# A two-layer encoder trunk: gate evacuation on ScalarE with the bias added on GpSimd, and an earlier hook for the next norm's transposes

## The chip, the cores and the metric

The kernel runs on one core of one Trainium2 chip. The metric is the device time of one execution in microseconds (us), the median of several runs. The engines are named as in the profile: PE (TensorE, with PEld for its weight loads), DVE (VectorE), ACT (ScalarE), POOL (GpSimd) and SP (SyncE, which issues DMAs here).

## The reference

Two layers, each a half-step feed-forward block, a mixer of three gated branches, and a second half-step feed-forward block, with a final norm at the end. All data is float32; the sequence has 256 tokens of 1024 channels. Cut to what matters here:

```python
for i in range(DEPTH):                      # DEPTH = 2
    h = rms_norm(x, ffn1_norm[i])
    x = x + 0.5 * swiglu_ffn(h, ffn1_w_gate[i], ffn1_w_up[i], ffn1_w_down[i])

    h = rms_norm(x, mix_norm[i])
    # one projection of h feeds three branches: S5, GLA, attention
    gates = jax.nn.sigmoid(h @ w_merge_gate[i] + b_merge_gate[i])     # 1024 x 3072
    gates = gates.reshape(bsz, seq_len, N_BRANCHES, D_MODEL)
    merged = (gates[:, :, 0] * (y_s5 @ w_branch_s5[i])
              + gates[:, :, 1] * (y_gla @ w_branch_gla[i])
              + gates[:, :, 2] * (y_attn @ w_branch_attn[i]))
    x = x + merged @ w_out[i]

    h = rms_norm(x, ffn2_norm[i])
    x = x + 0.5 * swiglu_ffn(h, ffn2_w_gate[i], ffn2_w_up[i], ffn2_w_down[i])
return rms_norm(x, final_norm)
```

## The kernel before

The 256 tokens are two tiles `t` of 128 partitions. Each large product is made of three matmuls (`mm3`, lines 219 to 221): activations and weights are each split into a rounded part and a remainder, and high times high, high times low and low times high are summed in PSUM. Weights are streamed: `load` fetches pieces of two times 128 rows by 512 columns into `raw`, ACT casts them to `hi` (L209), DVE subtracts to get `lo` (L210), and PE uses both. `raw`, `hi` and `lo` have five buffers each.

`stream` walks over weight blocks of 512 columns and over chunks of the contraction; when a block's last chunk is done, it calls the block's `evac` for both token tiles. `hooks` are calls put in after a chunk.

The norms are folded: `Norm.half` transposes x on PE (`pt`, L1127) and splits it into `hTh` and `hTl` without the root; each evacuation multiplies by the root `rstd`, one value for each token, that is for each partition.

In the mixer the main sequence (`MAIN`) runs input projection, the three gate streams g0, g1, g2, then the branch projections and the output projection `merge`. `weave` puts steps of the three branches between its chunks: these are the many small DVE, ACT and PE instructions around the gate streams (scans L790, L791, L908 and L909, products with tables L300, exponentials L920 and L921, transposes such as `goT`, L969, of the first GLA outputs). A gate block is evacuated by `ev` in `gate_stream`: DVE computes `ps * rstd + bm` (L714; `bm` is the bias, sent to all partitions by a DMA), ACT applies tanh in place (L715). A gate tile is 128 by 512; there are 12 in each mixer, 24 in the program.

The order on each engine is not that of the code. A scheduler places the instructions by a model of their times, and each engine then works through its own queue in that fixed order. An instruction that waits holds back all behind it on its engine.

## Time and profile before

| | |
|---|---|
| median of 3 runs | 1339.02 us (1336.95 to 1339.86) |
| profiled execution, its own time | 1340.2 us |
| its span, first to last instruction | 1338.4 us |
| granted TensorE clock, mean over the span | 0.996 |
| busy: PE, DVE, ACT, POOL | 1301.7, 1001.8, 700.9, 80.3 us |
| the two mixers' gate streams | about 320 to 397 us and 978 to 1055 us |

The busy sums are over the whole span. What matters for the change is the stretch of the gate streams, where the balance of the engines is another one than in the feed-forward blocks.

### The profile page before, as it was taken

How to read it: one execution, taken by the hardware profiler on the slowest of the kernel's cores; microseconds unless marked ns; L12 is line 12 of the kernel's file. 1: busy time of each engine (PE TensorE's matmuls, PEld its weight loads, DVE VectorE, ACT ScalarE, POOL GpSimd, SP SyncE). 2: the span in 40 equal slices, each digit the busy share in tenths (PEclk: the TensorE clock that was granted, in tenths of full speed). 3: DMA queues.
4: the chain of work that ended last, by engine and by line, in shares of the span. 5: the costliest groups of instructions: out<-in, count | busy, mean ns of one | idle time of the engine just before them, and what ended most of it. 6: DMA issues, size and time to landing. Idle time of an engine off the chain costs nothing.

```text
span 1338.4 us, 19258 instructions
## 1 busy us (share of the span) xinstructions
PE 1301.7 (97%) x6792; PEld 1050.6 (78%) x6792; DVE 1001.8 (75%) x1794; ACT 700.9 (52%) x1130; POOL 80.3 (6%) x108
## 2 busy tenths in 40 slices
PE   7999999999999999999999999999999999999997
PEld 5888778877787678888887888887787867788886
DVE  5899995779997769999556775557899966655553
ACT  5455444547675455544444454463485853645542
POOL 1010221000100000101000100000001000000000
PEclk9999999999999999999999999999999999999999
DMA  7766676676463367676656655576555525555561
GB/s 233 199 207 214 241 245 179 198 232 206 145 201 114 114 163 197 194 254 216 199 170 213 201 184 198 175 205 199 192 194 189 169 69 170 171 181 186 195 197 59
DMA packets 201200, 249.87 MB, mean 187 GB/s; under 512 B 40856, under 2 KB 134600, under 8 KB 201104
## 3 DMA queue, kind: packets, MB, share of 16 engines
q1 hardware_dynamic: 200496, 247.59, 59.1%
q8 instruction: 53, 0.87, 0.3%
q10 hardware_dynamic: 608, 1.06, 0.2%
q14 instruction: 43, 0.35, 0.1%
HBM read 234.44 MB, written 13.11 MB: 185 GB/s over the span
## 4 chain that ended last, share of the span: by engine, by line
PE 67%; issue 17%; DVE 11%; DMA 3%; POOL 1%; ACT 1%; SPq 0%; POOLq 0%; ACTq 0%; DVEq 0%
PE mm L219 19%; PE mm L221 19%; PE mm L220 19%; DVE lo L210 3%; DVE t L300 1%; DMA raw<-in_ffn_w_up 1%; PE S L773 1%; DMA e<-scr 1%; PE st L274 1%; PE as L1025 1%; PE ao L1047 1%; DVE run L791 1%; PE yp L811 1%; PE pt L1127 1%; PE apt L1040 1%
## 5 line engine op out<-in xcount | busy, mean ns | idle before, releaser
L210 DVE TENSOR_TENSOR lo<-raw,hi 128x1024 fp32r<-128x1024 f32 x412 | 499.4, 1218 | 203.6 <-ACT hi L209 193.6
L209 ACT CAST hi<-raw 128x1024 fp32r<-128x1024 f32 x412 | 427.8, 1043 | 330.2 <-PE mm L221 261.2
L219 PE MATMUL mm<-hi,hTh 128*128 128x512 f32 (+1 forms) x1120 | 441.8, 397 | 5.2 <-ACT hTh L1131 3.6
L220 PE MATMUL mm<-lo,hTh 128*128 128x512 f32 (+1 forms) x1120 | 441.1, 395 | 3.3 <-DVE lo L210 3.0
L221 PE MATMUL mm<-hi,hTl 128*128 128x512 f32 (+1 forms) x1120 | 429.7, 392 | 0.5 <-DVE hTl L1132 0.5
L219 PEld LDWEIGHTS mm<-hi,hTh 128*128 128x128 f32 x1120 | 211.1, 189 | 49.3 <-ACT hTh L1131 5.2
L220 PEld LDWEIGHTS mm<-lo,hTh 128*128 128x128 f32 x1120 | 211.5, 189 | 45.7 <-DVE lo L210 4.9
L221 PEld LDWEIGHTS mm<-hi,hTl 128*128 128x128 f32 x1120 | 210.9, 189 | 42.0 <-DVE hTl L1132 0.9
L220 PE MATMUL mm<-lo,sThffn 128*128 128x512 f32 x352 | 138.5, 394 | 2.2 <-DVE lo L210 2.2
L221 PE MATMUL mm<-hi,sTlffn 128*128 128x512 f32 x352 | 138.0, 393 | 0.0
L219 PE MATMUL mm<-hi,sThffn 128*128 128x512 f32 x352 | 137.1, 395 | 0.0
L220 PEld LDWEIGHTS mm<-lo,sThffn 128*128 128x128 f32 x352 | 66.5, 189 | 17.5 <-DVE lo L210 3.5
L219 PEld LDWEIGHTS mm<-hi,sThffn 128*128 128x128 f32 x352 | 66.6, 189 | 13.7
L221 PEld LDWEIGHTS mm<-hi,sTlffn 128*128 128x128 f32 x352 | 66.4, 189 | 14.0
L276 ACT CAST sThffn<-st 128x256 fp32r<-128x256 f32 x88 | 31.4, 373 | 73.0 <-PE st L274 72.6
L270 ACT ACTIVATE t<-mm,rstd 128x256 f32<-128x256 f32 x88 | 41.2, 473 | 49.0 <-PE mm L221 46.9
L277 DVE TENSOR_TENSOR sTlffn<-st,sThffn 128x256 fp32r<-128x256 f32 x88 | 35.8, 418 | 33.0 <-ACT sThffn L276 33.0
L271 DVE SCALAR_TENSOR_TENSOR t<-mm,rstd,t 128x256 f32<-128x256 f32 x88 | 41.0, 478 | 12.1 <-ACT t L270 11.8
L578 POOL COPY kx<-ks 128x128 f32<-128x128 f32 x32 | 24.0, 791 | 218.5 <-DVE ks L561 172.8
L300 DVE TENSOR_TENSOR t<-e,S 128x512 f32<-128x512 f32 x32 | 20.3, 682 | 15.0 <-DMA e<-scr 12.2
L274 PE MATMUL st<-ident,t 128*128 128x128 f32 x176 | 31.5, 273 | 0.0
L274 PEld LDWEIGHTS st<-ident,t 128*128 128x128 f32 x176 | 23.3, 140 | 9.1
(354 smaller groups left out, 1417.6 us busy)
## 6 DMA issues: line engine op xcount, KB each, us to landing
raw<-in_ffn_w_gate SPq DMA_DIRECT2D x176, 256.0 KB, 3.6
raw<-in_ffn_w_up SPq DMA_DIRECT2D x176, 256.0 KB, 3.8
raw<-in_ffn_w_down SPq DMA_DIRECT2D x88, 512.0 KB, 4.7
raw<-in_w_in SPq DMA_DIRECT2D x48, 512.0 KB, 3.8
raw<-in_w_merge_gate SPq DMA_DIRECT2D x48, 512.0 KB, 4.8
raw<-in_w_out SPq DMA_DIRECT2D x16, 512.0 KB, 3.8
scr<-e SPq DMA_DIRECT2D x6, 768.0 KB
e<-scr SPq DMA_DIRECT2D x6, 768.0 KB, 5.4
```

What stands on the lines that cost most here:

```text
L209: nc.scalar.copy(hi[:, :e - s, :width], raw[:, :e - s, :width])
L210: nc.vector.tensor_tensor(lo[:, :e - s, :width], raw[:, :e - s, :width], hi[:, :e - s, :width].bitcast(F32), op=ALU.subtract)
L219: nc.tensor.matmul(ps, act[0], w[0], start=first, stop=False)
L220: nc.tensor.matmul(ps, act[0], w[1], start=False, stop=False)
L221: nc.tensor.matmul(ps, act[1], w[0], start=False, stop=last)
L270: nc.scalar.activation(sg, ps[:, :256], AF.Silu, scale=rstd[:, t:t + 1])
L271: nc.vector.scalar_tensor_tensor(s, ps[:, 256:], rstd[:, t:t + 1], sg, op0=ALU.mult, op1=ALU.mult)
L274: nc.tensor.transpose(pt[:, j], s[:, j * P:(j + 1) * P], self.ident)
L276: nc.scalar.copy(h, pt)
L277: nc.vector.tensor_tensor(sl[:, 2 * b:2 * b + 2, t * P:(t + 1) * P], pt, h.bitcast(F32), op=ALU.subtract)
L300: self.nc.vector.tensor_tensor(out, a, b, op=ALU.mult)
L578: nc.gpsimd.tensor_copy(kx[:, :, s], ks.rearrange("p g j f -> p g (j f)")[:, :, (3 - s) * 16:(3 - s) * 16 + 64])
```

## The change

Three edits.

1. The gate's `scalar_tensor_tensor` on DVE is replaced by two instructions: ACT copies the PSUM tile with `rstd` as its scale, and POOL adds the bias in place. The tanh on ACT stays, and now waits for POOL.
2. The bias tile `bm` gets two buffers, where it had one.
3. `stream` also calls hooks with a key (chunk, sub-chunk), and the output projection's last hook, the first half of the next norm (`nm.half(0)`), is called after the first half of the last chunk's matmuls and no longer after all of them.

```diff
@@ stream
                 for t in range(NT):
                     for k in range(k0 + s, min(k1, k0 + s + SUB)):
                         self.mm3(ps[b, t][:, :width], act(k, t), w[k - k0], k == 0, k == nk - 1)
+                if (i, s) in hooks:
+                    hooks[i, s]()
             if i in hooks:
                 hooks[i]()
@@ gate_stream
-            bm = self.mp.tile([P, 512], F32, name=self.nm("bm"), tag="bm")
+            bm = self.mp.tile([P, 512], F32, name=self.nm("bm"), tag="bm", bufs=2)
...
                 g = gates[i][:, t, cs]
-                nc.vector.scalar_tensor_tensor(g, ps, rstd[:, t:t + 1], bm, op0=ALU.mult, op1=ALU.add)
+                nc.scalar.activation(g, ps, AF.Copy, scale=rstd[:, t:t + 1])
+                nc.gpsimd.tensor_tensor(g, g, bm, op=ALU.add)
                 nc.scalar.activation(g, g, AF.Tanh, scale=0.5)
@@ merge
-                               lead=2, hooks={0: lambda: mg.half(1), 3: lambda: nm.half(0)})
+                               lead=2, hooks={0: lambda: mg.half(1), (3, 0): lambda: nm.half(0)})
```

The scheduler sees the edits and places anew. Outside the mixers nothing moves. The lines of the changed kernel are two or three higher than before (L718 is the tanh there).

The first gate, on ACT, in the first mixer; `mm_3356` and `mm_3357` are the two token tiles of the first gate block, `gate_0` the gate. Before:

```order
L915 ACTIVATE mid_3160<-t_3157 128x1 x2
L814 COPY yg_2613<-yp_3215 128x2x4x16
L814 COPY yg_2613<-yp_3216 128x2x4x16
L918 ACTIVATE end_3161<-la_3077 128x1
L209 CAST hi_3721<-raw_3719 128x1024
L715 ACTIVATE gate_0_3339<-gate_0_3339 128x512
```

Now:

```order
L918 ACTIVATE mid_3160<-t_3157 128x1
L716 ACTIVATE gate_0_3339<-mm_3356,rstd_1795 128x512
L918 ACTIVATE mid_3160<-t_3157 128x1
L817 COPY yg_2613<-yp_3215 128x2x4x16
L817 COPY yg_2613<-yp_3216 128x2x4x16
L718 ACTIVATE gate_0_3339<-gate_0_3339 128x512
L921 ACTIVATE end_3161<-la_3077 128x1
L716 ACTIVATE gate_0_3339<-mm_3357,rstd_1795 128x512
L209 CAST hi_3725<-raw_3723 128x1024
```

The first tanh now stands ahead of the cast of the next weight piece (`hi_3721` before, `hi_3725` now), with only two short copies and one tiny activation between it and its evacuation; the second evacuation stands behind it.

DVE, some 25 us later in the same mixer, where the weight pieces of the second gate are made beside the S5 scans (L790 and L791 before, L793 and L794 now). Before:

```order
L714 SCALAR_TENSOR_TENSOR gate_0_3339<-mm_3525,rstd_1795,bm_3342 128x512
L210 TENSOR_TENSOR lo_3805<-raw_3802,hi_3804 128x1024
L210 TENSOR_TENSOR lo_3873<-raw_3870,hi_3872 128x1024
L303 TENSOR_TENSOR t_3322<-t_3322,t_3323 128x512
L306 TENSOR_TENSOR t_3324<-t_3324,t_3325 128x512
L210 TENSOR_TENSOR lo_3879<-raw_3876,hi_3878 128x1024
L985 TENSOR_REDUCE ass_3419<-t_3424 128x2
L790 SCALAR_TENSOR_TENSOR run_2590<-e_3305,t_3322 64x511
L791 SCALAR_TENSOR_TENSOR run_2590<-e_3305,t_3322 64x511
L300 TENSOR_TENSOR t_3416<-sp_3489,cst 128x256
L790 SCALAR_TENSOR_TENSOR run_2590<-e_3305,t_3324 64x511
L791 SCALAR_TENSOR_TENSOR run_2590<-e_3305,t_3324 64x511
```

Now:

```order
L793 SCALAR_TENSOR_TENSOR run_2590<-e_3305,t_3322 64x511
L794 SCALAR_TENSOR_TENSOR run_2590<-e_3305,t_3322 64x511
L793 SCALAR_TENSOR_TENSOR run_2590<-e_3305,t_3324 64x511
L794 SCALAR_TENSOR_TENSOR run_2590<-e_3305,t_3324 64x511
L210 TENSOR_TENSOR lo_3885<-raw_3882,hi_3884 128x1024
L988 TENSOR_REDUCE ass_3419<-t_3427 128x8
L302 TENSOR_TENSOR t_3416<-sp_3491,cst 128x256
L796 MEMSET run_2590 64x16
L797 MEMSET run_2590 64x16
L210 TENSOR_TENSOR lo_3982<-raw_3979,hi_3981 128x1024
```

The piece that was `lo_3879`, ahead of the scans, is now `lo_3885`, behind them; the piece after it (`lo_3976` before, `lo_3982` now) follows with a reduction and a small product between. The four gate instructions that stood ahead of the scans on DVE are gone.

PE, where the first GLA outputs are transposed (`goT_3400`). Before:

```order
L221 MATMUL mm_3883<-hi_3981,hTl_1798 128x512
L219 MATMUL mm_4074<-hi_4064,hTh_1797 128x512
L220 MATMUL mm_4074<-lo_4065,hTh_1797 128x512
L221 MATMUL mm_4074<-hi_4064,hTl_1798 128x512
L219 MATMUL mm_4074<-hi_4064,hTh_1797 128x512
L969 MATMUL goT_3400<-ident,t_3168 128x128 x2
```

Now:

```order
L220 MATMUL mm_3889<-lo_3885,hTh_1797 128x512
L221 MATMUL mm_3889<-hi_3884,hTl_1798 128x512
L221 MATMUL mm_3888<-hi_3981,hTl_1798 128x512
L972 MATMUL goT_3400<-ident,t_3168 128x128
L936 MATMUL keT_3487<-ident,la_3077 128x128
L972 MATMUL goT_3400<-ident,t_3168 128x128
```

The transposes stood at row 1525 of PE's queue and now stand at row 1503: 22 matmuls earlier, in the middle of the second gate's last chunk and no longer in the third gate's first.

The third edit moves nothing. Built with it and without it (the other two edits alike), the queues of all five engines have the same instructions at the same places; only the numbers in the names of the transposes' buffers differ (`pt_4812` with it, `pt_4824` without it). The eight transposes of x stand behind the last matmul of the output projection either way.

## Rows read from the trace of the kernel before

**Rows 1.** Page, busy us (share of the span) and instructions of each engine

```profile
PE 1301.7 (97%) x6792; PEld 1050.6 (78%) x6792; DVE 1001.8 (75%) x1794; ACT 700.9 (52%) x1130; POOL 80.3 (6%) x108
```

**Rows 2.** Windows: length, busy us of PE, PEld, DVE, ACT, POOL, clock

```profile
320.00:350.00 30.00, 30.00 (x184) 24.89 (x183) 29.66 (x44) 21.92 (x43) 0.54 (x1) 1.00 0.58 194
350.00:380.00 30.00, 27.61 (x161) 21.73 (x160) 29.76 (x49) 16.86 (x37) 4.26 (x2) 1.00 0.56 177
...
1007.00:1037.00 30.00, 27.58 (x161) 21.64 (x160) 29.79 (x48) 16.79 (x36) 4.24 (x2) 1.00 0.55 180
```

**Rows 3.** PE's waits, 320 to 370 us: total us, times, longest

```profile
PE mm L220 <- DVE lo L210: 1.5, 1, 1.5
PE mm L219 <- DVE gate L714: 0.8, 1, 0.8
```

**Rows 4.** Timeline of PE: start us, duration us, instruction, idle before

```profile
353.62 0.39 PE L221 MATMUL mm<-hi,hTl 128*128 128x512 f32 x1
353.85 0.39 PE L219 MATMUL mm<-hi,hTh 128*128 128x512 f32 x1
355.72 0.50 PE L220 MATMUL mm<-lo,hTh 128*128 128x512 f32 x1 [1.49 <-DVE lo L210]
...
366.46 0.38 PE L969 MATMUL goT<-ident,t 128*128 128x128 f32 x2
```

**Rows 5.** Timeline of DVE at the first gate

```profile
325.08 1.20 DVE L210 TENSOR_TENSOR lo<-raw,hi 128x1024 fp32r<-128x1024 f32 x1
...
326.53 1.22 DVE L210 TENSOR_TENSOR lo<-raw,hi 128x1024 fp32r<-128x1024 f32 x1
327.67 0.74 DVE L714 SCALAR_TENSOR_TENSOR gate<-mm,rstd,bm 128x512 f32<-128x512 f32 x1
328.33 0.42 DVE L306 TENSOR_TENSOR la<-t 128x256 f32<-128x256 f32 x1
...
329.32 1.21 DVE L210 TENSOR_TENSOR lo<-raw,hi 128x1024 fp32r<-128x1024 f32 x1
```

**Rows 6.** Timeline of DVE from the scans to the first GLA output

```profile
349.15 1.20 DVE L790 TENSOR_TENSOR_SCAN run<-e,t 64x511 f32<-64x511 f32 x1
...
355.58 0.68 DVE L985 TENSOR_REDUCE ass<-t 128x8 f32<-128x512 f32 x1
...
356.51 1.22 DVE L210 TENSOR_TENSOR lo<-raw,hi 128x1024 fp32r<-128x1024 f32 x1
...
363.69 0.61 DVE L966 SCALAR_TENSOR_TENSOR t<-go,grs,gs 128x128 f32<-128x128 f32 x2
```

**Rows 7.** Timeline of ACT at the first gate

```profile
324.45 0.20 ACT L915 ACTIVATE mid<-t 128x1 f32<-128x1 f32 x1
...
326.81 1.03 ACT L209 CAST hi<-raw 128x1024 fp32r<-128x1024 f32 x1
328.44 0.63 ACT L715 ACTIVATE gate<-gate 128x512 f32<-128x512 f32 x1 [0.60 <-DVE gate L714]
```

**Rows 8.** Groups by line: busy us, mean ns, idle before

```profile
L714 DVE SCALAR_TENSOR_TENSOR gate<-mm,rstd,bm 128x512 f32<-128x512 f32 x24 | 17.7, 745 | 0.0
...
L671 ACT ACTIVATE gs<-mm,rstd 128x512 f32<-128x512 f32 x2 | 1.4, 686 | 0.0
...
L568 POOL TENSOR_TENSOR e<-r,tcst 128x512 f32<-128x512 f32 x8 | 17.6, 2202 | 178.1 <-DVE r L300 105.1 <-DMA scr<-e 54.2 <-DVE T L316 11.1
```

**Rows 9.** Timeline of POOL and DVE, two executions of POOL's L568

```profile
157.70 2.65 POOL L568 TENSOR_TENSOR e<-r,tcst 128x512 f32<-128x512 f32 x1 [11.07 <-DVE T L316]
...
159.37 0.41 DVE L277 TENSOR_TENSOR sTlffn<-st,sThffn 128x256 fp32r<-128x256 f32 x1
159.71 1.73 DVE L210 TENSOR_TENSOR lo<-raw,hi 128x1024 fp32r<-128x1024 f32 x1
...
537.65 1.06 POOL L568 TENSOR_TENSOR e<-r,tcst 128x512 f32<-128x512 f32 x1 [48.00 <-DVE r L300]
...
537.70 1.07 DVE L319 TENSOR_TENSOR pt<-pw 128x32 f32<-128x32 f32 x1
```

## The prediction

> **What bounds the kernel now.** I began with the page: PE is busy 1301.7 of 1338.4 us [rows 1], so a change on DVE, ACT or POOL can shorten the time only by what PE waits, and lengthen it by any wait that it adds. Then I cut the gate streams into windows [rows 2]. From 320 to 380 us DVE is busy 29.66 and 29.76 of 30 us, ACT only 21.92 and 16.86, POOL 0.54 and 4.26; the second mixer reads the same (29.79 from 1007 to 1037 us). DVE is full there, and the edit takes work from it. But PE's waits in that stretch are small: 1.5 us for a `lo` and 0.8 us for a PSUM tile that a gate still holds [rows 3], 2.3 us in a mixer and 4.6 us in both. That is all that this stretch can give back. The wait for `lo` stands at 355.72 us, where PE had been ready since about 354.1 [rows 4].
>
> **What the change removes.** 24 gate instructions of 745 ns leave DVE [rows 8]. In DVE's full queue each is worth the step to the next start, 327.67 to 328.33 = 0.66 us [rows 5]; 12 in a mixer make 7.9 us. Four of them stand ahead of the late `lo`. DVE had no idle time before any gate [rows 8]: the tiles lie complete while DVE is behind, so ACT can take them at once, and PE's 0.8 us wait should go.
>
> **What it adds on ACT.** 24 copies from PSUM with a per-partition scale. The same form with the same shape is L671, 686 ns [rows 8]: 8.2 us in a mixer, and ACT has 8.1 and 13.1 us free in the two windows [rows 2]. As mere work this is hidden. It is the order that is not: ACT's first tanh stands between the first evacuation and the next cast, so while it waits for POOL, the second evacuation, the GLA steps and the cast of the next weight piece wait too, and behind that cast DVE's whole queue, whose next instruction is that piece's `lo`.
>
> **What it adds on POOL.** 24 adds of 128x512 with both inputs in SBUF. The nearest row is L568, a POOL TENSOR_TENSOR of that shape: 2202 ns on average over eight [rows 8], but 1.06 us where it was quick [rows 9]. The two executions shown tell why. At 157.70 POOL was ready, DVE was in a chain of products with two SBUF inputs, and POOL finished at 160.35: the work of 1.06 us can only have begun at about 159.3, when DVE came to L277 (159.37), whose one input is in PSUM. The DVE instruction after it, L210 with two SBUF inputs, then took 1.73 us, where it takes 1.20 to 1.22 elsewhere [rows 5, 9]; at 537.70 a small DVE product beside POOL took 1.07 us. I read from this that a POOL add waits while DVE runs two-input SBUF work without a gap, and that a DVE instruction of that kind waits while POOL adds. Bounds for the add's latency: 1.06 us, and several times that; for what it costs DVE: nothing (when DVE waits anyway or has a PSUM input) to about 0.9 us (537.70). I take 0.65 us where DVE is working, between 1.73 - 1.21 = 0.5 and 0.9. That is what the gate cost it before: **DVE's relief is paid back**.
>
> The Trainium skill's page "SBUF — State Buffer", section "Who interferes with whom", says that a DVE instruction with two SBUF inputs contends with a GpSimd instruction that reads SBUF, and that whoever issues first holds the shared ports for its whole instruction. The mutual hold agrees with rows 9; a wait of one instruction at most, as first come first served would have it, does not, since POOL stood behind more than one there. By the page's rule the first add would go in when the running `lo` ends at 326.3, DVE's next piece would start at 329.75, each later add would hold DVE for about 0.9, and the sum below would read 329.75 + 17.4 + 2.7 = 349.85 for the scans, 358.1 for `lo_3982` and 365.5 for L966: 4.1 us late in a mixer, +8 us in place of +5.7.
>
> **The sum, in the first mixer, on the clock of the rows.** ACT's first `mid` ends at 324.65 [rows 7], the evacuation at about 325.3. DVE then runs L909, `lo` (325.08), `la`, `lo` (326.53), `la`, all with two SBUF inputs, until about 328.0, when it needs the piece whose cast stands behind the tanh. Only now POOL gets in: add to 329.1, tanh to 329.75, `end` 0.1, second evacuation 0.6, cast 1.03 [rows 7]: DVE's next `lo` starts at 331.5. Before it started at 329.32 [rows 5]. From there to the scans DVE took 349.15 - 329.32 = 19.8 us [rows 5, 6]; take off two gates (1.3) and the `lo` that now follows the scans (1.14, the step 326.53 to 327.67): 17.4. Of adds 2 to 4, the second falls mostly into DVE's wait for the cast (0.2), the third holds a product for 0.65, and the fourth lies beside the products with S, which is in PSUM (0): 0.85. The scans begin at 331.5 + 17.4 + 0.85 = 349.75. Four scans of 1.21 [rows 6], the `lo` 1.15, the reduction and the small products 1.05, the next `lo` 1.15 bring `lo_3982` to 358.0. From that `lo`'s end (357.73) to the end of L966, the input of `goT`, DVE took 6.6 us before [rows 6]; without the two gates between and with one small copy moved in (0.3) it is 5.6, with one add held 6.25: ready at 364.3.
>
> Before, PE came to `goT` at 366.46 [rows 4]. It now stands 22 matmuls of 0.23 us [rows 4] earlier, so PE would be there at 361.4 with the waits it had. It is 364.3 - 361.4 = **2.9 us late**. After this point DVE again pays for each add what it saved, and PE has slack: no term, bounds 0 to +2 us, since the GLA and attention steps stand earlier in PE's queue than before. Two mixers: +5.7 us. The profiled execution took 1340.2 us, 1.2 above the median; on its own time this gives 1345.9, on the median **1344.7 us**.
>
> **Edits at nothing.** The third edit moves no instruction on any engine, so its price is nothing without any cover. The second bias buffer moves bias DMAs by a few places in SP's queue; a `bm` of 256 KB beside pieces of 512 KB is hidden by the casts, which were 2 us and more ahead of DVE (cast at 326.81, its `lo` at 329.32 [rows 5, 7]). If that cover were gone, a late piece would cost what a late `lo` costs, up to 1 to 2 us once.
>
> **Rivals.**
> *The relief works, faster (0.20).* If POOL finds a gap at once, the first add ends at 326.4, the tanh and what follows it lead to the `lo` at 328.6, the scans begin at 346.0, and L966 ends at 359.8, ahead of PE's 361.4. PE then gets back at most 1.6 us of its 2.3: -1.6 in a mixer, about -3.3 us, 1335.7. For it: two quick executions such as that at 537.65; that the gap of one instruction might do. Against: DVE is 99% busy just here, mostly with two SBUF inputs. It decides from a mean add of about 1.2 us downward.
> *Give and take, same (0.27).* The first add gets in at once, so that nothing waits behind its tanh, and the later ones hold DVE as in the sum (0.85 + 0.65): L966 ends at 359.8 + 1.5 = 361.3, PE finds `goT` ready as it comes, and the time stays at 1339.0. If all five later adds held DVE for 0.65, it would be 363.05, +1.6 in a mixer, 1342.3, where this case passes into the slower one. For it: with the first add alone hangs ACT's longest wait. Against: its place in DVE's densest chain.
> *Slower (0.53)*, my forecast, whose upper end adds the 2 us a mixer for the later steps: 1349 to 1350.
>
> **Numbers.** About 0.2% (2.7 us) is what a measurement of this kernel can tell from no change. Faster 0.20, same 0.27, slower 0.53. The range takes in the give-and-take case and nearly all of the faster one: 1335 to 1350; the slower case alone is 1342 to 1350.
>
> **What would show it.** In the profile after: the POOL add's mean near 2 us (quick case: 1.1); L210's mean above 1218 ns in the gate windows; ACT's tanh with idle time ended by POOL, the first one some 2 us; a DVE gap at about 328 us; PE waiting at `goT` for DVE, no longer for the gate's PSUM tile. Wrong, if the adds stay near 1.1 us and PE's waits there fall under 2.3 us; or if PE stalls more at attention's transposes, which I priced at nothing.

## The result, and the profile after

The changed kernel takes **1359.53 us** (median of 4 runs, 1358.23 to 1362.5), the kernel before 1338.56 in the same comparison: a ratio of 1.0157, 95% interval 1.0145 to 1.0169, or 21 us more. The forecast was 1344.7 us with a range of 1335 to 1350: the sign was right, the forecast loss was less than a third of the one that came, and the time lies outside the range. The profiled execution took 1362.5 us, its span is 1360.7 us, its mean granted clock 0.992.

The page's busy times, which answer to [rows 1]:

```profile
PE 1311.4 (96%) x6792; PEld 1053.3 (77%) x6792; DVE 999.8 (73%) x1770; ACT 714.7 (53%) x1154; POOL 127.0 (9%) x132
```

PE has the same 6792 instructions. DVE lost 24, but only 2 us of busy time, where 24 gates of 745 ns [rows 8] are 17.9: the rest came back as longer instructions. The groups by line (busy us, mean ns, idle time ahead and what ended it), which answer to [rows 8]:

```profile
L717 POOL TENSOR_TENSOR gate<-gate,bm 128x512 f32<-128x512 f32 x24 | 39.7, 1666 | 179.4 <-ACT gate L716 179.3
...
L990 POOL TENSOR_TENSOR ars<-ass,mhalf 128x20 f32<-128x20 f32 x2 | 17.2, 8598 | 4.9 <-DVE ass L989 4.9
...
L716 ACT ACTIVATE gate<-mm,rstd 128x512 f32<-128x512 f32 x24 | 16.2, 682 | 3.0 <-PE mm L221 3.0
L718 ACT ACTIVATE gate<-gate 128x512 f32<-128x512 f32 x24 | 15.1, 630 | 17.3 <-POOL gate L717 17.2
...
L302 DVE TENSOR_TENSOR qk<-qk,ars 128x512 f32<-128x512 f32 (+1 forms) x8 | 7.7, 1025 | 6.9 <-POOL ars L990 6.9
```

The add has a mean of 1666 ns, ACT stands 17.2 us in front of its tanh for POOL, and a row that the prediction did not speak of has grown: `ars`, attention's root, a power over 128x20 on POOL, takes 8.6 us, with 6.9 us of idle time on DVE behind it. Before, it took 3.5 us, and no engine stood for it:

```profile
L987 POOL TENSOR_TENSOR ars<-ass,mhalf 128x20 f32<-128x20 f32 x2 | 7.1, 3534 | 8.8 <-DVE ass L986 8.8
```

The same windows as [rows 2], three short ones after them and one of the second mixer (busy us of PE, PEld, DVE, ACT, POOL; then the granted clock), and, after the line of dots, the kernel before from 380 to 410 us:

```profile
320.00:350.00 30.00, 27.98 (x165) 22.82 (x162) 26.53 (x39) 22.70 (x45) 8.94 (x5) 1.00 0.56 174
350.00:380.00 30.00, 24.36 (x139) 18.05 (x137) 26.37 (x39) 14.26 (x31) 15.26 (x6) 0.99 0.35 110
380.00:384.00 4.00, 2.97 (x12) 2.68 (x13) 3.90 (x9) 3.97 (x8) 0.00 (x0) 0.50 0.75 259
384.00:388.00 4.00, 4.00 (x18) 3.71 (x17) 4.00 (x11) 4.00 (x11) 0.00 (x0) 0.50 0.57 181
388.00:392.00 4.00, 4.00 (x17) 3.18 (x16) 4.00 (x10) 3.61 (x8) 0.88 (x1) 0.79 0.77 214
1034.00:1038.00 4.00, 3.86 (x18) 2.72 (x19) 4.00 (x9) 3.52 (x7) 3.50 (x1) 0.60 0.74 229
...
380.00:410.00 30.00, 30.00 (x183) 26.14 (x182) 27.69 (x55) 26.11 (x54) 1.43 (x2) 1.00 0.55 178
```

From 320 to 380 us PE is busy 52.3 us where it was 57.6, and DVE 52.9 where it was 59.4: both now wait. Then PE's clock is at half (0.50 of 2.4 GHz) for 8 us and more, where it was at 1.00 before. PE's waits, 320 to 370 us as in [rows 3], and after the line of dots 370 to 400 us:

```profile
PE goT L972 <- DVE t L969: 1.9, 1, 1.9
PE sp L942 <- DVE t L302: 1.3, 1, 1.3
PE mm L220 <- DVE lo L210: 0.9, 2, 0.7
PE yp L811 <- DVE t L946: 0.5, 1, 0.5
PE mm L219 <- ACT gate L716: 0.4, 1, 0.4
PE keT L936 <- ACT la L932: 0.2, 1, 0.2
...
PE go L958 <- ACT gst L953: 1.7, 1, 1.7
PE mm L220 <- DVE lo L210: 1.0, 1, 1.0
PE yTp L824 <- ACT yg L820: 0.7, 1, 0.7
```

The first six make 5.2 us against 2.3 in [rows 3]: 2.9 more. The last three are new, 3.4 us; from 370 to 400 us PE waited for nothing before. The timeline of the changed kernel at both places, engine by engine (start, duration, instruction, idle time ahead), which answers to [rows 5, 7]:

```profile
324.16 3.92 POOL L717 TENSOR_TENSOR gate<-gate,bm 128x512 f32<-128x512 f32 x1 [73.72 <-ACT gate L716]
...
364.45 8.60 POOL L990 TENSOR_TENSOR ars<-ass,mhalf 128x20 f32<-128x20 f32 x1 [2.44 <-DVE ass L989]
373.02 2.99 POOL L717 TENSOR_TENSOR gate<-gate,bm 128x512 f32<-128x512 f32 x2
...
328.12 0.63 ACT L718 ACTIVATE gate<-gate 128x512 f32<-128x512 f32 x1 [3.55 <-POOL gate L717]
...
374.35 0.63 ACT L718 ACTIVATE gate<-gate 128x512 f32<-128x512 f32 x1 [3.17 <-POOL gate L717]
379.07 0.69 ACT L932 ACTIVATE la<-t,end 128x128 f32<-128x128 f32 x2 [4.09 <-DVE t L302]
...
325.38 1.22 DVE L210 TENSOR_TENSOR lo<-raw,hi 128x1024 fp32r<-128x1024 f32 x1
326.51 0.42 DVE L308 TENSOR_TENSOR la<-t 128x256 f32<-128x256 f32 x1
330.39 1.48 DVE L210 TENSOR_TENSOR lo<-raw,hi 128x1024 fp32r<-128x1024 f32 x1 [3.46 <-ACT hi L209]
...
348.45 1.20 DVE L793 TENSOR_TENSOR_SCAN run<-e,t 64x511 f32<-64x511 f32 x1
...
363.70 0.60 DVE L969 SCALAR_TENSOR_TENSOR t<-go,grs,gs 128x128 f32<-128x128 f32 x2
...
368.97 0.68 DVE L305 TENSOR_TENSOR t<-t,t 128x512 f32<-128x512 f32 x1
373.09 3.08 DVE L302 TENSOR_TENSOR qk<-qk,ars 128x512 f32<-128x512 f32 x2 [3.44 <-POOL ars L990]
```

At the first gate: POOL's add is ready at 324.16 and its work (1.29 us where nothing is in the way) ends at 328.08, 1.15 us after the end of DVE's chain at 326.93; ACT's tanh waits 3.55 us, the cast behind it is late, DVE idles 3.46 us. Forty us later the same pair meets again in the other order: `ars` stands behind DVE's chain until 373.05, and two things stand behind `ars`: DVE's products `qk` and POOL's own next adds, for which ACT waits 3.17 us and then 4.09 us more for a product that DVE does after `qk`. PE's three new waits are the ends of these two chains.

### The profile page after: what moved, and what is told of

Read it like the earlier page. It is cut to its first block, busy times and chain, and to the rows that moved or that the text cites. A ratio compares the mean times of both kernels' runs of the same rounds, so it can differ in the third digit from the quotient of the medians.

```text
span 1360.7 us, 19265 instructions
## 1 busy us (share of the span) xinstructions
PE 1311.4 (96%) x6792; PEld 1053.3 (77%) x6792; DVE 999.8 (73%) x1770; ACT 714.7 (53%) x1154; POOL 127.0 (9%) x132
## 4 chain that ended last, share of the span: by engine, by line
PE 57%; issue 19%; DVE 14%; ACT 4%; POOL 3%; DMA 3%; SPq 0%; ACTq 0%; POOLq 0%; DVEq 0%
PE mm L221 17%; PE mm L219 16%; PE mm L220 16%; DVE lo L210 3%; DVE t L302 2%; DMA e<-scr 1%; POOL ars L990 1%; DVE run L794 1%; ACT hi L209 1%; DVE run L793 1%; POOL gate L717 1%; PE as L1028 1%; PE ao L1050 1%; PE st L276 1%; DMA raw<-in_ffn_w_up 1%
## 5 line engine op out<-in xcount | busy, mean ns | idle before, releaser
L219 PE MATMUL mm<-hi,hTh 128*128 128x512 f32 (+1 forms) x1120 | 443.5, 398 | 4.2 <-ACT hTh L1134 3.4
L221 PE MATMUL mm<-hi,hTl 128*128 128x512 f32 (+1 forms) x1120 | 429.7, 393 | 1.2 <-DVE hTl L1135 1.2
L219 PEld LDWEIGHTS mm<-hi,hTh 128*128 128x128 f32 x1120 | 211.7, 189 | 48.5 <-ACT hTh L1134 5.0
L221 PEld LDWEIGHTS mm<-hi,hTl 128*128 128x128 f32 x1120 | 211.3, 189 | 43.1 <-DVE hTl L1135 1.6
L221 PE MATMUL mm<-hi,sTlffn 128*128 128x512 f32 x352 | 137.3, 391 | 0.0
L219 PE MATMUL mm<-hi,sThffn 128*128 128x512 f32 x352 | 136.4, 393 | 0.0
L221 PEld LDWEIGHTS mm<-hi,sTlffn 128*128 128x128 f32 x352 | 66.1, 188 | 13.8
L219 PEld LDWEIGHTS mm<-hi,sThffn 128*128 128x128 f32 x352 | 66.1, 188 | 13.6
L717 POOL TENSOR_TENSOR gate<-gate,bm 128x512 f32<-128x512 f32 x24 | 39.7, 1666 | 179.4 <-ACT gate L716 179.3
L580 POOL COPY kx<-ks 128x128 f32<-128x128 f32 x32 | 20.1, 669 | 219.6 <-DVE ks L563 146.8
L570 POOL TENSOR_TENSOR e<-r,tcst 128x512 f32<-128x512 f32 x8 | 17.9, 2236 | 178.4 <-DMA scr<-e 62.5
```

What stands on the lines that cost most here:

```text
L219: nc.tensor.matmul(ps, act[0], w[0], start=first, stop=False)
L221: nc.tensor.matmul(ps, act[1], w[0], start=False, stop=last)
L717: nc.gpsimd.tensor_tensor(g, g, bm, op=ALU.add)
```

## The experiments

The theories. **A**: POOL is kept waiting by DVE's chain of instructions with two SBUF inputs, and what queues behind POOL, on ACT above all, pays. **B**: ACT's added work costs. **C**: the adds hold DVE while they run. **D**: the new order on PE, or POOL's own queue, costs. **E**: DVE's relief is worth nothing on the path. The expectations name them by these letters. All results but those of three spoilt runs, which follow further down:

| run | median us | ratio to before, 95% interval |
|---|---|---|
| changed kernel | 1359.53 | 1.0157 (1.0145 to 1.0169) |
| hookonly | 1338.62 | 1.0004 (0.9989 to 1.0018) |
| relief_clean | 1340.36 | 1.0006 (0.9995 to 1.0017) |
| no_add_clean | 1339.51 | 0.9991 (0.9980 to 1.0002) |
| add_dve | 1345.05 | 1.0041 (1.0027 to 1.0054) |
| tiny_add | 1347.48 | 1.0069 (1.0047 to 1.0092) |
| one_input_clean | 1352.11 | 1.0084 (1.0068 to 1.0100) |
| tanh_late | 1362.75 | 1.0170 (1.0144 to 1.0196) |
| tanh_dep | 1355.11 | 1.0125 (1.0103 to 1.0148) |
| tiny_dep | 1343.82 | 1.0016 (1.0002 to 1.0031) |
| ars_gap | 1359.56 | 1.0147 (1.0127 to 1.0168) |
| add_gap | 1364.87 | 1.0193 (1.0174 to 1.0211) |
| b_spare_adds | 1352.27 | 1.0102 (1.0071 to 1.0134) |
| spare_one_input | 1344.89 | 1.0035 (1.0022 to 1.0048) |
| g0_pool | 1356.64 | 1.0124 (1.0107 to 1.0141) |
| g1_pool | 1354.94 | 1.0113 (1.0098 to 1.0128) |

**The third edit alone** (hookonly, in the kernel before).

```diff
-lead=2, hooks={0: lambda: mg.half(1), 3: lambda: nm.half(0)})
+lead=2, hooks={0: lambda: mg.half(1), (3, 0): lambda: nm.half(0)})
```

> The third edit alone: the kernel before with the next norm's first transposes called after the first piece of the output projection's last chunk instead of after the whole chunk. All theories: no instruction changes its place on any engine, so 1338 to 1341 us, an interval that holds 1. If that edit has any part in the 21 us, it shows here.

Measured 1.0004: it has no part in the 21 us.

**Nothing in place of DVE's gate** (relief_clean, in the kernel before), and **ACT's evacuation without an add** (no_add_clean, in the changed kernel):

```diff
-nc.vector.scalar_tensor_tensor(g, ps, rstd[:, t:t + 1], bm, op0=ALU.mult, op1=ALU.add)
-nc.scalar.activation(g, g, AF.Tanh, scale=0.5)
+nc.scalar.activation(g, ps, AF.Tanh, bias=bm[:, :1], scale=rstd[:, t:t + 1])
...
-nc.scalar.activation(g, ps, AF.Copy, scale=rstd[:, t:t + 1])
-nc.gpsimd.tensor_tensor(g, g, bm, op=ALU.add)
+nc.scalar.activation(g, ps, AF.Identity, bias=bm[:, :1], scale=rstd[:, t:t + 1])
```

> The run that leaves DVE's gate out once more, now with the bias row still loaded and read (one column of it is tanh's bias; the rest of the bias and the factor of a half are left out of the output), so that its loads keep their places in SP's queue. DVE has 24 instructions of 0.66 us less to do, ACT and POOL no more than before, and TensorE's order is close to that of the changed kernel. Theory E (DVE's relief falls where nobody waits for DVE, so it is worth nothing, and the order that comes with it costs nothing either): 1336 to 1342 us. If the relief is worth what the prediction set against the adds' hold: 1326 to 1335 us. If it is the new order of TensorE's instructions that costs (theory D): 1345 us and more.

> The same for the run without an add: ACT evacuates with the root as scale and one column of the bias row as bias (the rest of the bias is left out of the output), so the row's loads stay where they are; nothing on POOL. It has ACT's 24 more instructions and DVE's relief and no station on POOL. Theory E with ACT's work hidden: 1338 to 1343 us. Rival B (ACT's added evacuations are the cost): over 1350 us.

Both intervals hold 1. Taking 24 instructions off an engine that is 99% busy in this stretch, with the new order that comes of it, gives nothing back, and 24 evacuations more on ACT cost nothing on top. That a gain of the relief and a cost of the order cancel is not excluded: the runs show their sum. E holds in this sense; B falls, and so does D as far as it is the order. All of the 21 us hang on POOL's add. In the window from 350 to 380 us of no_add_clean, PE has 29.54 us of work, against 27.61 before [rows 2] and 24.36 after, at full clock:

```profile
350.00:380.00 30.00, 29.54 (x178) 23.66 (x177) 29.81 (x57) 22.76 (x46) 4.26 (x2) 1.00 0.51 161
380.00:390.00 10.00, 10.00 (x52) 8.35 (x51) 9.09 (x19) 9.79 (x19) 0.70 (x1) 1.00 0.44 148
```

Three earlier runs of these questions are spoilt: relief_only (1358.75 us, ratio 1.0141), no_add (1343.3, 1.0025) and one_input (1352.41, 1.0089) left the bias row without a reader, its loads moved together in SP's queue, and weights queued behind them. SP's waits in relief_only, 215 to 250 us:

```profile
SPq L710 <- DMA bm<-in_b_merge_gate: 16.3, 5, 3.8
```

PE then stood 7.4 us at 242 us, ahead of any gate; that those loads are the reason was not shown, as the profile names nothing that ended this wait. What the three were to show is read from the clean ones, which differ from them in that they read one column of the row:

```diff
-nc.scalar.activation(g, ps, AF.Tanh, scale=rstd[:, t:t + 1])
+nc.scalar.activation(g, ps, AF.Tanh, bias=bm[:, :1], scale=rstd[:, t:t + 1])
...
-nc.scalar.activation(g, ps, AF.Copy, scale=rstd[:, t:t + 1])
+nc.scalar.activation(g, ps, AF.Identity, bias=bm[:, :1], scale=rstd[:, t:t + 1])
...
-nc.gpsimd.tensor_scalar(g, g, 0.0, 1.0, op0=ALU.add, op1=ALU.mult)
+nc.gpsimd.tensor_scalar(g, g, bm[:, :1], 1.0, op0=ALU.add, op1=ALU.mult)
```

> The kernel before with DVE's gate instruction left out and nothing put in its place: ACT's tanh reads PSUM with the root as its scale (bias and the factor of a half are left out of the output). DVE is relieved of 24 instructions of 0.66 us, ACT and POOL have no more to do than before. It is the most that taking the gates off DVE could bring. If DVE's relief is worth what the prediction set against the adds' hold (7.9 us of DVE a mixer, of which some 3 to 6 us were on the path): 1326 to 1335 us. If the relief falls where nobody waits for DVE (theory E: only holds are on the path, and freed time is not): 1336 to 1342 us.

> The changed kernel without the bias add on POOL: ACT still takes every gate out of PSUM and still does tanh, nobody adds the bias (the output lacks it). Theory A (POOL waits for a gap between DVE's instructions with two SBUF inputs, and what queues behind POOL waits too): the 3.9 us first add and ACT's 3.6 us idle time ahead of the first tanh go, goT's data is back at or before 364 us and PE waits under 1 us there; the ars power at 364 us is still shut out, because DVE's chain has no gate in it either way, so its 8.6 us and the PE waits behind it stay: 1348 to 1354 us. Rival B (ACT's 24 more evacuations and their place in ACT's queue are the cost, whatever POOL does): within 3 us of the changed kernel, 1357 to 1361 us. Rival C (the adds slow DVE down while they run): DVE's lo at L210 falls from 1224 ns to about 1190 ns in the mean and the time to 1335 to 1342 us.

> The changed kernel with POOL's add of gate and bias replaced by an instruction of the same 512 columns with one SBUF input (add 0, times 1; the bias is left out of the output). POOL still stands between ACT's evacuation and tanh for some 0.5 to 1.5 us. If the cost comes from two engines that each read two SBUF tiles (theory A's wait for a gap, rival C's hold of DVE), both go: the first one ends within 2 us, no DVE instruction at L210 or L302 takes over 1.4 us beside one, and the time is 1341 to 1348 us, near that without an add. If it is the station on POOL as such, whatever it reads (its length and the two hand-overs), the time stays at 1352 to 1360 us.

**The add on DVE** (add_dve).

```diff
-nc.gpsimd.tensor_tensor(g, g, bm, op=ALU.add)
+nc.vector.tensor_tensor(g, g, bm, op=ALU.add)
```

> The changed kernel with the bias add on DVE instead of POOL: ACT takes the gate out of PSUM, DVE adds the bias between two SBUF tiles (0.68 us by the 128x512 adds at L308), ACT does tanh. DVE's work is then as before the change, ACT's as after it. Theory A: no add is shut out, so ACT's 3.6 us idle time ahead of the first tanh falls under 2 us, but the ars power meets a DVE chain that holds two SBUF inputs throughout and still takes over 7 us: 1349 to 1356 us. Rival B (ACT's work): 1357 to 1361 us. Rival C (POOL's adds slow DVE): 1338 to 1342 us.

Measured 1345.05 us, between the expectations of A and C; B is out. The expected row came: POOL's power was shut out even longer than in the changed kernel, and DVE stood for it,

```profile
361.70 9.72 POOL L990 TENSOR_TENSOR ars<-ass,mhalf 128x20 f32<-128x20 f32 x1 [6.01 <-DVE ass L989]
...
371.46 1.70 DVE L302 TENSOR_TENSOR qk<-qk,ars 128x512 f32<-128x512 f32 x4 [3.09 <-POOL ars L990]
```

and yet the whole kernel lost only 5.5 us. A late `ars` by itself is cheap.

**A gap for `ars`** (ars_gap) and **gaps for the adds** (add_gap).

```diff
 nc.gpsimd.tensor_tensor(rs, ss, self.mhalf[:, :20], op=ALU.pow)
+gap = self.t2([P, 8])
+nc.vector.tensor_reduce(gap, qk[:, 0, 0:8], axis=AX.X, op=ALU.add)
...
 nc.gpsimd.tensor_tensor(g, g, bm, op=ALU.add)
+with self.tc.high_priority():
+    nc.vector.tensor_reduce(self.st.tile([P, 1], F32, name=self.nm("gp"), tag="gp"), ps, axis=AX.X, op=ALU.add)
```

> The changed kernel with one needless instruction more on DVE: a tensor_reduce with one SBUF input (128x512 to 128x8, some 0.6 us) right after the instruction at L989 that feeds the ars power on POOL, so that POOL can start its power beside it. Theory A (POOL's power waits about 5 us until DVE leaves a gap): although DVE has more to do, ars takes 3 to 4 us instead of 8.6 in both mixers, DVE's 3.4 us idle time before qk (L302) goes, and PE's 4.4 us of waits between 376 and 383 us fall under 2; with them the stretch of half clock right behind shortens: 1345 to 1354 us. Rival B (ACT's work) and rival C (the adds slow DVE): ars as long as before or shorter, the time within 2 us of the changed kernel or 1 us above it, 1358 to 1361 us.

> The changed kernel with 24 needless instructions more on DVE: for each gate a tensor_reduce that reads the gate's tile in PSUM (128x512 to 128x1, some 0.6 us, nobody reads its result), at nearly the places at which DVE's gate instructions stood before the change. DVE's work is then that of the kernel before, and POOL's adds stay. If POOL waits for DVE to leave its chain of instructions with two SBUF inputs (theory A), the needless instructions let the adds and the ars power in: the ars power takes under 5 us instead of 8.6, and the time falls by 3 us or more though DVE has 15.8 us more to do, 1346 to 1356 us; only the first add, whose needless instruction stands behind the chain, still takes over 3 us. If DVE's load or the adds' own length is what costs: 1360 to 1375 us.

The mechanism came, the gain did not. In ars_gap POOL's power went in beside the one-input reduction and took 3.54 us, but now the two adds behind it stood 6.71 us, and ACT behind them:

```profile
366.11 3.54 POOL L990 TENSOR_TENSOR ars<-ass,mhalf 128x20 f32<-128x20 f32 x1 [2.43 <-DVE ass L989]
370.73 6.71 POOL L717 TENSOR_TENSOR gate<-gate,bm 128x512 f32<-128x512 f32 x2 [1.09 <-ACT gate L716]
...
375.80 0.63 ACT L718 ACTIVATE gate<-gate 128x512 f32<-128x512 f32 x1 [2.99 <-POOL gate L717]
```

In add_gap `ars` took 3.92 us, and the time rose by 5 us over that of the changed kernel. The long `ars` is thus not the cause that I took it for at first: with it gone another instruction of POOL's stands in the same place, and the adds still hold DVE (its scan L796, 1.22 us alone, took 2.14).

**The tanh elsewhere in the code** (tanh_late: moved from `gate_stream` to `branch`, ahead of its use).

```diff
-nc.scalar.activation(g, g, AF.Tanh, scale=0.5)
...
+nc.scalar.activation(g, g, AF.Tanh, scale=0.5)
 nc.vector.scalar_tensor_tensor(g, g, 1.0, ps, op0=ALU.add, op1=ALU.mult)
```

> The changed kernel with each gate's tanh moved from right behind the add to the place where the gate is used, so that nothing on ACT waits for POOL's add in the stream of gate blocks. Theory A with the head-of-line wait on ACT as its main part: ACT's second evacuation and the casts behind it start some 3 us earlier, DVE's lo is back at 329.5 us instead of 330.4, PE's wait at goT falls from 2.0 us to under 1: 1353 to 1357 us; the ars power is untouched at about 8.6 us. If the head-of-line wait is not on the path: 1358 to 1361 us. Rival B (ACT's work itself, its order no matter): 1358 to 1361 us.

The scheduler placed the instructions of every engine as in the changed kernel, and the time is that of the changed kernel. The run tells nothing on the wait; it shows that moving code is not moving an instruction.

**A short instruction on POOL** (tiny_add: 8 columns; one_input_clean: 512 columns, one full SBUF input).

```diff
-nc.gpsimd.tensor_tensor(g, g, bm, op=ALU.add)
+nc.gpsimd.tensor_tensor(g[:, :8], g[:, :8], bm[:, :8], op=ALU.add)
...
+nc.gpsimd.tensor_scalar(g, g, bm[:, :1], 1.0, op0=ALU.add, op1=ALU.mult)
```

> The changed kernel with POOL's add cut from 512 columns to the first 8 (the bias of the others is left out): the same stations ACT, POOL, ACT for each gate, with next to no work in the middle one. If it is the wait for a gap between DVE's two-input instructions that costs (theory A), the first add still does not end before DVE's chain does, ACT stays idle some 2.5 to 3.5 us ahead of its first tanh, the ars power stays over 7 us, and the time stays at 1350 to 1358 us. If it is the add's own length (1.3 us alone, and what it takes from DVE while it runs; rival C), the time falls to that without an add, 1340 to 1346 us.

> The same for POOL's instruction with one full SBUF input: gate plus one column of the bias row (the rest of the bias is left out of the output), 128x512, some 0.63 us long where it is not kept waiting, in place of the add with two full inputs at 1.3 us and more. The row's loads stay where they are. If two inputs on each side are what costs: within 5 us of the run without an add. If the station on POOL costs even so (the first instruction still waits 3 us behind DVE's chain, as the first such run showed): 1346 to 1352 us, between the run without an add and the changed kernel.

Both cost, 9 and 11 to 13 us: tiny_add fell between its two expectations (its `ars` took 4.4 us and not over 7), one_input_clean came out at the upper end of its second. The first POOL instruction of tiny_add, and below it that of one_input_clean with its second:

```profile
324.04 2.83 POOL L717 TENSOR_TENSOR gate<-gate,bm 128x8 f32<-128x8 f32 x1 [71.51 <-ACT gate L716]
328.61 0.20 POOL L717 TENSOR_TENSOR gate<-gate,bm 128x8 f32<-128x8 f32 x1 [1.75 <-ACT gate L716]
```

```profile
322.82 3.31 POOL L717 TENSOR_SCALAR gate<-gate,bm 128x512 f32<-128x512 f32 x1 [73.19 <-ACT gate L716]
327.56 0.70 POOL L717 TENSOR_SCALAR gate<-gate,bm 128x512 f32<-128x512 f32 x1 [1.43 <-ACT gate L716]
```

The second execution is the instruction alone, the first the same with its wait: 2.83 - 0.20 = 2.63, 3.31 - 0.70 = 2.61, and in the changed kernel 3.92 - 1.29 = 2.63 us. The wait is that of DVE's chain and does not ask how long POOL's instruction is, nor whether it reads one SBUF tile or two. Nor is it a slow start of POOL after 70 us without work: the first add of tanh_dep took 2.11 us after 72 us, and the first spare instruction of spare_one_input 1.04 us after 82 us (both runs follow). That is A's part, and it is there with next to no add.

**Adds that nobody waits for** (b_spare_adds, and spare_one_input with one input, both in the kernel before, with every order on PE as before).

```diff
 nc.vector.scalar_tensor_tensor(g, ps, rstd[:, t:t + 1], bm, op0=ALU.mult, op1=ALU.add)
+nc.gpsimd.tensor_tensor(sp, bm, bm, op=ALU.add)
...
+nc.gpsimd.tensor_scalar(sp, bm, 0.0, 1.0, op0=ALU.add, op1=ALU.mult)
```

> The kernel before, with 24 adds more on POOL that nobody waits for (bias plus bias into a spare tile, 128x512, two SBUF inputs, one for each gate), all else and the order of TensorE's and ACT's instructions as before. It has the contention of POOL's adds with DVE without their place in the gate's chain. Theory A: DVE's gates read PSUM, so POOL finds its gaps; at most the ars power is delayed by an add ahead of it: 1339 to 1344 us. Rival C (the adds hold DVE up): 24 times 0.65 us, up to 1354 us, with DVE's lo (L210) above 1218 ns in the mean.

> The kernel before with 24 spare instructions on POOL that nobody waits for, as in the run with spare adds, but with one SBUF input (bias row plus 0, 128x512) in place of two. All orders on TensorE, ACT and DVE as before. The run with two inputs cost about 14 us, with single DVE instructions held by 0.6 to 0.8 us. If the hold comes from both engines reading two SBUF tiles: 1338 to 1342 us and no DVE instruction held over 0.4 us. If any POOL work there costs (POOL's own queue, the scans behind it): 1345 us and more.

Here C is right: 14 us (the runs spread from 1347.56 to 1354.88; the profiled one is the fastest) and 5 to 6 us, between the two cases expected, with no consumer at all. POOL's own queue (D) is not it: from 300 to 410 us no engine waits for POOL in either run. Two adds of b_spare_adds beside the scans, and DVE's rows there:

```profile
346.77 3.25 POOL L716 TENSOR_TENSOR sp<-bm 128x512 f32<-128x512 f32 x2 [9.28 <-DMA bm<-in_b_merge_gate]
...
347.33 1.86 DVE L792 TENSOR_TENSOR_SCAN run<-e,t 64x511 f32<-64x511 f32 x1
349.20 1.90 DVE L793 TENSOR_TENSOR_SCAN run<-e,t 64x511 f32<-64x511 f32 x1
...
352.71 1.22 DVE L793 TENSOR_TENSOR_SCAN run<-e,t 64x511 f32<-64x511 f32 x1
```

Two scans took 0.64 and 0.68 us more than the 1.22 of the last. PE's wait for the `lo` behind the scans was 3.0 us instead of 1.5 [rows 3].

**The two parts taken apart** (tanh_dep, tiny_dep). A bias column of zeros, made from the branch's input, holds each tanh back until its branch begins, so that ACT waits for no add; in tiny_dep the add is also cut to 8 columns. Every engine has the same instructions in the same order in these two, but for the add's width.

```diff
+z = self.st.tile([P, 1], F32, name=self.nm("zb"), tag="zb")
+nc.scalar.activation(z, yl[:, 3, SEQ - 1:SEQ].bitcast(F32), AF.Copy, scale=0.0)
...
+nc.scalar.activation(g, g, AF.Tanh, bias=z, scale=0.5)
 nc.vector.scalar_tensor_tensor(g, g, 1.0, ps, op0=ALU.add, op1=ALU.mult)
```

> The changed kernel with each tanh held back until its branch's input is complete, by a bias column of zeros that is made from that input; four tanh then stand together ahead of the branch's block, and nothing in ACT's queue waits for POOL while the gate blocks run. POOL's adds are as starved as before, but nobody waits for them. Theory A (the cost is what stands behind the starved add in ACT's queue: second evacuation, casts, la, gst): ACT's 3.6 us ahead of the first tanh and its 3.2 us at 371 us go, the ars power stays long: 1341 to 1349 us. Rival C (the adds slow DVE while they run) and rival D (POOL's adds push back POOL's own powers, ars above all): 1354 to 1361 us.

> Both cuts at once: the add on POOL only 8 columns wide (the bias of the others is left out of the output) and each tanh held back until its branch's input is complete, so that ACT waits for no add while the gate blocks run. Every engine has the same instructions in the same order as in the run with late tanh alone, but for the width of the add. If the cost has two parts, what waits behind the add on ACT (the 9 us of the run with the narrow add) and what the full add takes from DVE while it runs (the 12 us more of the full one), both are gone: 1338 to 1343 us. If the narrow add's 9 us come from POOL's own queue (the ars power behind it) and not from ACT's wait: 1345 to 1350 us. If the late tanh itself costs, as four of them stand ahead of each branch: 1345 us and more, with ACT's tanh rows ahead of TensorE's waits at the branches.

tanh_dep came out at 1355.11 us, where C and D had it and not A; tiny_dep at 1343.82, just above what was expected if the two parts are all. With late tanh the full add costs 1.25%, the narrow one 0.16%, about 15 us between them that are the add's width alone. `ars` took 3.5 us in both, and no engine stands for POOL for more than 0.3 us from 300 to 410 us, so POOL's own queue (D) falls here too. DVE at the first gate in tanh_dep, and then the same place in tiny_dep:

```profile
324.05 1.19 DVE L210 TENSOR_TENSOR lo<-raw,hi 128x1024 fp32r<-128x1024 f32 x1
325.17 1.51 DVE L308 TENSOR_TENSOR la<-t 128x256 f32<-128x256 f32 x1
```

```profile
324.43 1.20 DVE L210 TENSOR_TENSOR lo<-raw,hi 128x1024 fp32r<-128x1024 f32 x1
325.54 0.42 DVE L308 TENSOR_TENSOR la<-t 128x256 f32<-128x256 f32 x1
```

`la` takes 0.42 us alone and 1.51 beside a full add: a hold of 1.1 us, nearly the add's whole length. With the narrow add the wait for the tanh is worth 7 us (ratios 1.0069 and 1.0016), with the full add some 4 us (1.0157 and 1.0125; their intervals just touch).

**One gate's add on POOL, the others on DVE** (g0_pool, g1_pool).

```diff
-nc.gpsimd.tensor_tensor(g, g, bm, op=ALU.add)
+(nc.gpsimd if i == 0 else nc.vector).tensor_tensor(g, g, bm, op=ALU.add)
```

> The changed kernel with POOL's add for the first gate only (8 of 24 adds); the second and third gate's bias is added on DVE. Beside the kernel with all adds on DVE (5.5 us slower than before) it has the 3.9 us first add with ACT's idle time behind it, and PE's later wait at goT: plus 4 to 8 us by theory A, 1348 to 1353 us; by rival C (each add costs alike by what it holds of DVE) a third of the 15 us that separate all adds on POOL from all on DVE, 1349 to 1351 us. Together with the next run it shows where in the mixer the cost lies.

> The changed kernel with POOL's add for the second gate only (8 of 24 adds), the others on DVE: those that stand beside the ars power and DVE's chain of two-input instructions. Theory A (place decides: starved POOL beside ars, ACT's la and gst behind the tanh): plus 6 to 11 us on the kernel with all adds on DVE, 1351 to 1356 us. Rival C (each add costs alike): 1349 to 1351 us. If the cost needs the first gate's delay to build on: 1344 to 1347 us.

Measured 1356.64 and 1354.94 us. Against add_dve (ratio 1.0041) that is 11 and 9.5 us for 8 adds each, and 15.5 us for all 24: the costs don't add up. The first gate's came out above both expectations, the second gate's within A's. The scheduler's order on PE is not the same in these kernels, and its part in the difference was not taken apart. A third of the adds on POOL already brings most of the loss, so there is no cheap place for them among the first two gates; the third was not tried alone.

**Where in the mixer.** The matmuls of the streams (L219 to L221) come in nearly the same order in these kernels (at most 106 of 4896 stand elsewhere), so the start of the n-th of them can be compared. Late against before, in us, counted from the 1120th (at 307.4 us before); the 1320th starts some 5 us behind `goT`, the 1360th starts at 376.2 us before, the 1520th at 446.4:

| first mixer | 1320th | 1360th | 1520th |
|---|---|---|---|
| no_add_clean | -0.8 | 2.3 | 0.0 |
| tiny_dep | -0.4 | 3.2 | 1.1 |
| tiny_add | 1.8 | 6.4 | 4.0 |
| one_input_clean | 2.5 | 8.8 | 6.5 |
| tanh_dep | 4.2 | 10.5 | 8.5 |
| ars_gap | 4.9 | 11.9 | 10.7 |
| changed kernel | 5.0 | 16.2 | 13.8 |

PE's other work stands earlier in the new order, so part of each row at the 1360th (2.3 us without an add) is given back by the 1520th. Between the marks PE does the same work in no_add_clean and in the changed kernel: from the 1120th to the 1320th 57.4 and 63.1 us, from there to the 1360th 13.7 and 21.9, to the 1520th 67.9 and 67.9. So the first mixer lost 5.7 us up to the 1320th and **8.2 us in the 40 matmuls after it**, in the stretch behind `goT` for which the prediction had no term. Of the 8.2 most can be read: PE's three waits there make 3.4 us, and PE worked some 8.7 us at half clock behind them (2.97 and 4.00 us of the windows with 0.50, and two fifths of the window with 0.79), which costs about 4.3, an estimate from those rows.

The second mixer lost 10.5 us. Counted to `goT` itself, the changed kernel falls behind no_add_clean by 5.5 us in the first mixer and 5.1 in the second (from the 1120th matmul to `goT` 57.9 against 52.4 us, and 57.4 against 52.3), and by 8.3 and 5.4 us after it. The second mixer had the half clock too, but shorter (0.60 from 1034 to 1038 us). How much of it there is differs from execution to execution: tanh_late, with the same order on every engine, lost 12.6 and 13.0 us in its two mixers.

## Why the prediction was wrong in size

- **What bounds the kernel** was read rightly: PE had 2.3 us of waits to give back in a mixer, and the relief of DVE could bring no more. With no add, PE's waits up to `goT` fell to 0.7 us, and the program was still no faster (no_add_clean; relief_clean likewise).
- **ACT's added work is hidden**: right (no_add_clean). **The third edit is worth nothing**: right (hookonly). The second bias buffer was not tried alone, but no_add_clean has it and loses nothing.
- **The add on POOL waits for DVE's chain, and ACT, the cast and DVE's next piece wait behind it**: right, close to its numbers. The add ended at 328.08 (329.1 forecast), DVE's next `lo` started at 330.39 (331.5), the scans at 348.45 (349.75), and `goT`'s input was ready at 364.3 (364.3). The profiled execution stood 1.2 us ahead of the kernel before at the 1120th matmul (306.2 and 307.4), so on the clock of the forecast the first three are right within 0.2 us, and the last is 1.2 us late. The sum had one add held there, for 0.65 us; two held DVE, for 0.9 and 1.1 (the product takes 0.68 and the `lo` 1.21 alone):

```profile
359.28 1.59 DVE L302 TENSOR_TENSOR t<-e,run 128x512 f32<-128x512 f32 x1
360.79 2.31 DVE L210 TENSOR_TENSOR lo<-raw,hi 128x1024 fp32r<-128x1024 f32 x1
```

So PE began `goT` at 364.09, which is 365.3 on that clock, 3.9 us behind the 361.4 of the forecast and not 2.9. That its waits up to there rose by the 2.9 us of the sum all the same is luck: the wait at `goT` was 1.9, and a net 1.0 came at places that the sum did not look at, with 1.3 us at `sp`. The add's mean of 1666 ns lies below the "near 2 us" that was to show this.

- **The step that failed** is the next one: "After this point DVE again pays for each add what it saved, and PE has slack: no term, bounds 0 to +2 us." After that point the first mixer lost 8.3 us more than the kernel without an add, and the second 5.4. PE's slack there was read from a kernel in which `ars` takes 3.5 us; in the changed one `ars`, which the prediction did not price, and the second gate's adds stand in one POOL queue beside DVE's chain, ACT's and DVE's next steps stand behind them, and PE waited for both and then worked at half clock, for which the sum had no term either.
- **Behind that stands the netting**, "DVE's relief is paid back". It is true of DVE's busy time (999.8 us against 1001.8). It is no balance on the path: the freed 0.66 us a gate, with the order that comes of them, are worth nothing, as relief_clean shows, while a hold lengthens just the instruction that the next engine waits for, as b_spare_adds and tanh_dep against tiny_dep show. The single hold was put at 0.65 us, bounds 0 to 0.9; 0.64 to 1.1 us came.
- **The rivals.** *The relief works* had the add's quick end as its point of decision; even with no add at all there is no gain, so its 1335.7 us could not be reached. *Give and take* falls with the first add's wait. But tanh_dep comes near its condition, the first add in after 0.8 us and nothing queued behind it, and still loses 17 us: the holds alone, put at a balance with the relief, are not one.
- **The rule of the skill.** By the Trainium skill's page "SBUF — State Buffer", section "Who interferes with whom", the first to issue holds the shared ports for its whole instruction. That DVE instructions are held for almost an add's length agrees (1.1 of 1.29 us). Read as first come, first served, as the prediction read it, the waiting engine would get in after the running instruction. That agrees with tanh_dep's first add, which took 2.11 us, 0.8 of it a wait; it does not agree with the 2.63 us behind four DVE instructions in the changed kernel. The measurement decides for both: neither case can be counted on. The +8 us of that reading fall short of the 21 us as well.

How the 21 us split into wait and hold stays partly open, since the two parts don't add: over the kernel before, the narrow late add costs 2 us, the narrow one in its place 9, the full late one 17, and both parts together 21. That POOL's station is the whole cause, and that each part costs without the other, is shown.

## What to carry over

An engine that is full is not yet an engine whose relief pays: run the kernel with the work left out before planning where to move it, and keep every load that the left-out work would have read. Work put on POOL beside a dense chain of two-input DVE instructions cost twice here: by what waits for POOL and by what POOL holds; price both at every POOL instruction in the stretch, old ones such as `ars` too, and follow each queue past the first wait to the next one.

## What the runs showed of the hardware that was not expected

- POOL's wait behind DVE's chain was the same 2.6 us for instructions of 0.20, 0.70 and 1.29 us, with one SBUF input or two; in one other kernel (tanh_dep), at the same instructions of DVE, it was 0.8.
- POOL's power over 128x20 took 3.53 to 9.72 us, by what DVE did beside it, and 3.54 when a reduction with one SBUF input was put there.
- After PE's waits of 1.0 and 1.7 us near 377 to 380 us the granted clock stood at 0.50, 1.2 GHz, from 380 to 388 us; in the kernel without an add, whose PE waited for no more than 0.5 us there, it was 1.00 throughout from 350 to 390. Such a wait does not always do it: behind one of 2.5 us at 373 us in g0_pool the clock stayed at 1.00 up to 390.
